# A decoder trunk on one core: attention scores three heads ahead, and products with the values behind the next head's transposes, first parts first

## The chip, the cores and the metric

The kernel runs on one core of one Trainium2 chip. Times are device microseconds of one execution. The core has five engines that each run their own instructions in a fixed order: TensorE (PE, matmuls; PEld are its weight loads), VectorE (DVE), ScalarE (ACT), GpSimd (POOL) and SyncE (SP, which issues the DMA transfers).

## The reference, cut to what matters

The program is a trunk of two decoder layers over 512 positions of width 1024. The first layer mixes a gated MLP (half A) and eight heads of stick-breaking attention (half B), projects both halves with one matrix, and is followed by a squared-ReLU MLP; the second layer uses an mLSTM. The change is in the attention of the first layer only:

```python
def _stick_breaking(q, k, v):              # (1, 8 heads, 512, 64)
    scale = q.shape[-1] ** -0.5
    for blk in range(seq // 128):
        t0, t1 = blk * 128, blk * 128 + 128
        z = jnp.einsum('bhtd,bhsd->bhts', q[:, :, t0:t1], k[:, :, :t1]) * scale
        mask = jnp.arange(t1)[None, :] < jnp.arange(t0, t1)[:, None]
        log1m = jnp.where(mask, -jax.nn.softplus(z), 0.0)
        suffix = lax.cumsum(log1m, axis=3, reverse=True)
        a = jnp.where(mask, jnp.exp(z + suffix), 0.0)
        outs.append(jnp.einsum('bhts,bhsd->bhtd', a, v[:, :, :t1]))

def _even_mixer(h, w_in, w_out, ...):
    ...                                     # y_a: gated MLP; q, k normed, v from p = h @ w_in
    o = _stick_breaking(q, k, v)
    return jnp.concatenate([y_a, y_b], axis=-1) @ w_out
```

## The kernel before

Everything is in float32. A matmul operand is carried as two parts, a first part `hi` (written by ACT) and a second part `lo`, the rest (written by DVE as source minus `hi`); a product is then three matmuls (`mm3`: hi by hi, lo by hi, hi by lo), and the helper `split` makes the parts. Weights come by DMA in tiles of 128 x 1024 (`w_load`), are split by ACT (`wh`, L189) and by DVE or, for tiles 14 to 29, by POOL (`wl`, L190), and five split tiles are held.

The attention works head by head. `head_scores(h)` transposes q (for two heads at once) and k into PSUM banks of tag B and splits them into `qs`, `kh` and `kl`; then, for the four blocks of 128 queries from the last to the first, it forms the scores `z` in a B bank (L530 to L532). ACT takes two sigmoids of it: `m`, of minus z (L535), and `a`, of z (L536). DVE runs a product scan backwards over `m` (L537) and multiplies `a` by the shifted scan (L540; by DVE for the last block of queries, by POOL for the other three). For a head the scans are 512, 384, 256 and 128 wide.

`head_out(h, aa)` then transposes the pieces of `a` into banks of tag C (L554), in three steps: key block j = 0, j = 1, and j = 2 and 3 together. Each step is split into `hi` and `lo` (L286, L287). These parts lie in two sets of buffers: even heads use three blocks of `xhi` and `xlo`, odd heads `ath1` and `atl1`. The products with the values go to the one bank of tag O (L567), for each key block the first part and then the second. The output is gathered (`ot`, L573 and L574) and split once more: the first part by ACT (L576), the second, `yl`, by POOL (L577).

While attention runs, PE is given filler work: `w_out_pieces` multiplies half A, which is ready, by the output matrix, in 32 pieces of three matmuls (banks of tag A, operands `yah` and `yal`); after every four pieces, that is twelve matmuls, DVE adds the finished block to the residual `xres` (L587). The function `step`, called behind certain matmuls of the attention, counts a quarter for each call, and at every full one it issues a piece. What is left over runs behind the attention, ahead of the product of half B with the output matrix (operands `vc`, `xlo`, `xhi`).

The calls are written in this order: scores of heads 0 and 1, the V projection, then for each head the scores of the next but one head and the output of this one. A scheduler that runs when the program is built takes the written order as priorities and fixes the order on each engine; where operands or buffers are not free, work that was written later can stand earlier.

Of the kernel before, what the change touches and what calls it, by code (L numbers as in the profile page):

```python
# [12 lines left out]
F32 = mybir.dt.float32  # L13
# [6 lines left out]
P = 128  # L20
T = 512
NT = 4
# [110 lines left out]
def _program(ctx, tc, nc, I, O):  # L133
    pool = lambda n, b=1: ctx.enter_context(tc.tile_pool(name=n, bufs=b))
    act, dve, pe, gp = nc.scalar, nc.vector, nc.tensor, nc.gpsimd
    f = lambda t: t.bitcast(F32)
# [9 lines left out]
    def bank(tag, dt=F32):  # L146
        cnt[0] += 1
        return ps.tile([P, 512], dt, name=f"ps{tag}{cnt[0]}", tag=f"ps{tag}", bufs=NB[tag])
# [86 lines left out]
    def w_take(n, la=LA):  # L235
        a = wpos[0]
        wpos[0] += n
        while len(wq) < wpos[0] + la:
            if next(units, units) is units:
                break  # L240
        return wq[a:a + n]
# [13 lines left out]
    def tts(t):  # L255
        return slice(t * P, (t + 1) * P)
# [24 lines left out]
    def split_scaled(dhi, dlo, src, g):  # L281
        act.activation(dhi, src, AF.Copy, scale=g)
        dve.scalar_tensor_tensor(dlo, src, g, f(dhi), op0=ALU.mult, op1=ALU.subtract)  # L283

    def split(dhi, dlo, src):
        act.activation(dhi, src, AF.Copy)  # L286
        dve.tensor_tensor(dlo, src, f(dhi), op=ALU.subtract)  # L287
# [161 lines left out]
    with ExitStack() as ax:  # L449
        ap = ax.enter_context(tc.tile_pool(name="at", bufs=1))  # L450
        qn = [ap.tile([P, 512], F32, name=f"qn{t}") for t in range(NT)]
        kn = [ap.tile([P, 1024], F32, name=f"kn{t}") for t in range(NT)]
        vc = ap.tile([P, NT, 8, 2, 64], F32R, name="vc")
# [4 lines left out]
        AO = (0, 512, 896, 1152)  # L458
        fl = lambda a: a[:, 0:3, :].rearrange("p k t -> p (k t)")
        ath = [fl(xhi), ap.tile([P, 1408], F32R, name="ath1")]  # L460
        atl = [fl(xlo), ap.tile([P, 1408], F32R, name="atl1")]
# [26 lines left out]
        def tok_transpose(src, c0):  # L488
            c = bank("B")
            for t in range(NT):  # L490
                i = pe.transpose(c[:, tts(t)], src[t][:, c0:c0 + P], ident)
            step(i)
            return c
# [5 lines left out]
        def step(ins):  # L499
            acc[0] += RATE if fill else 0  # L500
            if acc[0] >= 1:
                acc[0] -= 1
                with tc.issue_after(ins.ins):
                    next(fill[0], None)

        def head_scores(h):
            if h % 2 == 0:
                c = tok_transpose(qn, h * 64)
                for e in range(2):
                    es = slice(64 * e, 64 * e + 64)  # L510
                    qs = ap.tile([P, 512], F32R, name=f"qs{h + e}", tag="qs", bufs=3)
                    act.activation(qs[:64], c[es], AF.Copy, scale=pc("qng")[es])
                    dve.scalar_tensor_tensor(qs[64:], c[es], pc("qng")[es], f(qs[:64]), op0=ALU.mult, op1=ALU.subtract)
                    qst[h + e] = qs
            qs = qst[h]
            c = tok_transpose(kn, h * P)
            kh = ap.tile([P, 512], F32R, name=f"kh{h}", tag="kh", bufs=2)
            kl = ap.tile([P, 512], F32R, name=f"kl{h}", tag="kl", bufs=2)
            split_scaled(kh, kl, c, kng8)
            aa = [None] * NT  # L520
            z01 = None
            for tb in (3, 2, 1, 0):
                if tb > 1:
                    z = bank("B")
                else:
                    z01 = z01 if z01 is not None else bank("B")
                    z = z01[:, tb * 256:(tb + 1) * 256]
                n = P * (tb + 1)
                w = max(n, 256)
                pe.matmul(z[:, :w], lhsT=qs[:, tts(tb)], rhs=kh[:, :w], start=True, stop=False)  # L530
                pe.matmul(z[:, n - P:n], lhsT=identb, rhs=maskb[:, :P], start=False, stop=False)
                step(pe.matmul(z[:, :w], lhsT=qs[:, tts(tb)], rhs=kl[:, :w], start=False, stop=True))  # L532
                m = ap.tile([P, n], F32, name=f"m{h}_{tb}", tag=f"m{tb}", bufs=1)
                a = ap.tile([P, n], F32, name=f"a{h}_{tb}", tag=f"a{tb}", bufs=2)
                act.activation(m, z[:, :n], AF.Sigmoid, scale=-1.0)  # L535
                act.activation(a, z[:, :n], AF.Sigmoid)  # L536
                dve.tensor_tensor_scan(m[:, ::-1], m[:, ::-1], ones.to_broadcast([P, n]), 1.0,  # L537
                                       op0=ALU.mult, op1=ALU.mult)
                eng = dve if tb == 3 else gp
                eng.tensor_tensor(a[:, :n - 1], a[:, :n - 1], m[:, 1:n], op=ALU.mult)  # L540
                aa[tb] = a
            return aa
# [1 line left out]
        ones = ap.tile([P, 1], F32, name="ones")  # L544
        gp.memset(ones, 1.0)

        def head_out(h, aa):
            hi, lo = ath[h % 2], atl[h % 2]
            for js in ((0,), (1,), (2, 3)):
                c = bank("C")  # L550
                n = 0
                for j in js:
                    for tb in range(j, NT):
                        i = pe.transpose(c[:, n:n + P], aa[tb][:, j * P:(j + 1) * P], ident)  # L554
                        n += P
                step(i)
                if len(js) == 1:
                    split(hi[:, AO[j]:AO[j] + n], lo[:, AO[j]:AO[j] + n], c[:, :n])
                else:
                    split(hi[:, 896:1152], lo[:, 896:1152], c[:, :256])  # L560
                    split(hi[:, 1280:1408], lo[:, 1280:1408], c[:, 256:384])
            o = bank("O")
            for j in range(NT):
                t0 = min(j, 2) * P
                v2 = vc[:, j, h].rearrange("p e d -> p (e d)")
                for i, w in enumerate((hi, lo)):
                    x_ = pe.matmul(o[:, t0:], lhsT=v2, rhs=w[:, AO[j]:AO[j] + T - t0], start=j == 0 and i == 0,  # L567
                                   stop=j == NT - 1 and i == 1)
                step(x_)
            pr = slice((h % 2) * 64, (h % 2) * 64 + 64)  # L570
            yh, yl = yb(h // 2, 0)[pr], yb(h // 2, 1)[pr]
            ot = junk.tile([P, T], F32, name=f"ot{h}", tag="jk", bufs=1)[pr]
            act.activation(ot, o[64:], AF.Copy)  # L573
            dve.tensor_tensor(ot, o[:64], ot, op=ALU.add)  # L574
            oc = ot.rearrange("p (t c) -> p t c", t=NT)
            act.activation(yh, oc, AF.Copy)  # L576
            gp.tensor_tensor(yl, oc, f(yh), op=ALU.subtract)  # L577

        def w_out_pieces(hus):

            for d in range(KT):
                for k in range(4):
# [4 lines left out]
                        dve.tensor_tensor(xs[:, d, :], b, xs[:, d, :], op=ALU.add)  # L587
                    yield

        pend = [head_scores(0), head_scores(1)]  # L590
        act_chunk(w_take(4, LAV), 2, 512, v_evac, itertools.cycle("A"))
        pieces = w_out_pieces(w_take(4, 0))
        fill[:] = [pieces]
        for a in ath + atl:
            gp.memset(f(a[:, 1152:1280]), 0.0)
        for h in range(8):
            if 2 <= h + 1 < 8:
                pend.append(head_scores(h + 1))
            head_out(h, pend.pop(0))
        fill.clear()  # L600
        for _ in pieces:
            pass
# [336 lines left out]
```

## Time and profile before

| | |
|---|---|
| median of 3 runs | 1137.15 us (1135.97 to 1138.31) |
| profiled execution | 1138.17 us, its span 1136.4 us |
| PE busy | 1105.9 us (97%), 6372 matmuls |
| DVE busy | 825.9 us (73%) |
| ACT busy | 523.9 us (46%) |
| POOL busy | 163.9 us (14%) |
| granted PE clock | 0.994 over the span |

Rows of the timeline give the start in the span, the duration, engine, line, operation, the tiles written and read, shapes, and in brackets how long the engine stood idle before and what ended that. A matmul's duration holds its pipeline, so the distance from one start to the next is what it costs in a run of matmuls. Where a row is marked x2, two operations of one form are merged.

### The profile page before, as it was taken

How to read it: one execution, taken by the hardware profiler on the slowest of the kernel's cores; microseconds unless marked ns; L12 is line 12 of the kernel's file. 1: busy time of each engine (PE TensorE's matmuls, PEld its weight loads, DVE VectorE, ACT ScalarE, POOL GpSimd, SP SyncE). 2: the span in 40 equal slices, each digit the busy share in tenths (PEclk: the TensorE clock that was granted, in tenths of full speed). 3: DMA queues.
4: the chain of work that ended last, by engine and by line, in shares of the span. 5: the costliest groups of instructions: out<-in, count | busy, mean ns of one | idle time of the engine just before them, and what ended most of it. 6: DMA issues, size and time to landing. Idle time of an engine off the chain costs nothing.

```text
span 1136.4 us, 15912 instructions
## 1 busy us (share of the span) xinstructions
PE 1105.9 (97%) x6372; PEld 959.9 (84%) x6372; DVE 825.9 (73%) x1135; ACT 523.9 (46%) x800; POOL 163.9 (14%) x154
## 2 busy tenths in 40 slices
PE   7899989999999999999999999999999999999998
PEld 5788767878988988988988888887899899899898
DVE  7753599468957957857977677679887677677685
ACT  5343577445435435435555444435543444444441
POOL 7316564540000000000030010003100000000000
PEclk9899999999999999999999999999999999999999
DMA  7222310242241241251042203204324224224121
GB/s 231 92 75 76 105 43 1 74 169 91 94 133 71 97 138 64 93 149 56 20 130 77 93 20 112 93 25 155 118 74 140 83 74 147 76 75 149 37 84 65
DMA packets 34506, 105.18 MB, mean 93 GB/s; under 512 B 3712, under 2 KB 10112, under 8 KB 34432
## 3 DMA queue, kind: packets, MB, share of 16 engines
q1 hardware_dynamic: 34432, 104.17, 28.4%
q8 instruction: 50, 0.82, 0.3%
q14 instruction: 24, 0.20, 0.1%
HBM read 102.06 MB, written 2.10 MB: 92 GB/s over the span
## 4 chain that ended last, share of the span: by engine, by line
PE 79%; DVE 13%; ACT 2%; issue 2%; POOL 2%; DMA 2%; SPq 0%; DVEq 0%; ACTq 0%; POOLq 0%
PE psA L292 10%; PE psA L290 10%; PE psA L291 10%; PE psB L676 7%; PE psB L674 7%; PE psB L675 7%; PE psC L291 5%; PE psC L292 5%; PE psC L290 5%; DVE m L537 2%; DVE wl L190 2%; PE psO L290 2%; PE psO L291 2%; PE psO L292 2%; DVE xlo L283 1%
## 5 line engine op out<-in xcount | busy, mean ns | idle before, releaser
L189 ACT ACTIVATE wh<-wr 128x1024 fp32r<-128x1024 f32 (+1 forms) x124 | 131.3, 1061 | 173.3 <-DMA wr<-wall 53.1
L190 DVE TENSOR_TENSOR wl<-wr,wh 128x1024 fp32r<-128x1024 f32 (+1 forms) x108 | 136.6, 1271 | 84.4 <-ACT wh L189 54.2
L189 ACT ACTIVATE wh<-wq_s 128x1024 fp32r<-128x1024 f32 x64 | 67.2, 1060 | 125.3 <-PE psC L291 57.8
L291 PE MATMUL psA<-xlo,wh 128*128 128x512 f32 x292 | 115.2, 394 | 0.0
L292 PE MATMUL psA<-xhi,wl 128*128 128x512 f32 x288 | 114.1, 396 | 0.5 <-DVE wl L190 0.5
L290 PE MATMUL psA<-xhi,wh 128*128 128x512 f32 x288 | 112.6, 392 | 1.1 <-DVE xres L327 1.1
L291 PE MATMUL psC<-xlo,wh 128*128 128x512 f32 x256 | 102.1, 399 | 0.0
L292 PE MATMUL psC<-xhi,wl 128*128 128x512 f32 x256 | 102.0, 399 | 0.0
L290 PE MATMUL psC<-xhi,wh 128*128 128x512 f32 x256 | 101.2, 395 | 0.0
L292 PE MATMUL psA<-wh,xlo 128*128 128x512 f32 (+2 forms) x232 | 87.7, 380 | 4.0 <-DVE xlo L283 2.2
L290 PE MATMUL psA<-wh,xhi 128*128 128x512 f32 (+2 forms) x232 | 88.4, 383 | 1.8 <-ACT wh L189 1.7
L189 ACT ACTIVATE wh<-wq 128x1024 fp32r<-128x1024 f32 x48 | 50.9, 1060 | 85.2 <-PE psB L675 35.1
L291 PE MATMUL psA<-wl,xhi 128*128 128x512 f32 (+2 forms) x232 | 87.7, 379 | 1.1 <-DVE wl L190 1.1
L190 DVE TENSOR_TENSOR wl<-wq_s,wh 128x1024 fp32r<-128x1024 f32 x64 | 77.5, 1219 | 3.5 <-ACT wh L189 2.5
L339 POOL TENSOR_TENSOR ssq<-ssq,sq 128x512 f32<-128x512 f32 x18 | 28.8, 1600 | 351.8 <-ACT sq L338 351.8
L725 DVE SCALAR_TENSOR_TENSOR r<-psC,rrow 128x512 f32<-128x512 f32 x32 | 22.1, 690 | 60.8 <-PE psC L292 60.8
L290 PEld LDWEIGHTS psA<-xhi,wh 128*128 128x128 f32 x288 | 54.7, 190 | 13.8 <-ACT sq L338 1.5
L291 PEld LDWEIGHTS psA<-xlo,wh 128*128 128x128 f32 x292 | 54.9, 188 | 12.2
L686 DVE TENSOR_TENSOR xres<-xres,psB 128x512 f32<-128x512 f32 x80 | 53.9, 681 | 15.4 <-PE psB L676 14.8
L292 PEld LDWEIGHTS psA<-xhi,wl 128*128 128x128 f32 x288 | 54.1, 188 | 12.2 <-DVE wl L190 0.8
L190 DVE TENSOR_TENSOR wl<-wq,wh 128x1024 fp32r<-128x1024 f32 x48 | 58.6, 1221 | 2.6 <-ACT wh L189 2.3
L290 PEld LDWEIGHTS psC<-xhi,wh 128*128 128x128 f32 x256 | 48.9, 191 | 11.1
(396 smaller groups left out, 3147.4 us busy)
## 6 DMA issues: line engine op xcount, KB each, us to landing
wr<-wall SPq DMA_DIRECT2D x122, 512.0 KB, 3.5
wq<-wall SPq DMA_DIRECT2D x64, 512.0 KB, 3.9
out<-xres SPq DMA_DIRECT2D x16, 128.0 KB, 1.8
wr<-wv SPq DMA_DIRECT2D x2, 528.0 KB, 3.5
xres<-xT SPq DMA_DIRECT2D x4, 256.0 KB, 5.7
xres<-xT SPq DMA_DIRECT2D x2, 512.0 KB, 8.6
lngb<-lngb SPq DMA_DIRECT2D x1, 512.0 KB, 5.4
sgr<-sgw SPq DMA_DIRECT2D x1, 512.0 KB, 6.2
```

Of the source, the lines that this page charges most:

```text
L189: act.activation(hi[:, :n], raw, AF.Copy)
L190: (gp if i in POOL_LO else dve).tensor_tensor(lo[:, :n], raw, f(hi[:, :n]), op=ALU.subtract)
L290: pe.matmul(out, lhsT=lh, rhs=rh, start=first, stop=False)
L291: pe.matmul(out, lhsT=lh, rhs=rl, start=False, stop=False)
L292: pe.matmul(out, lhsT=ll, rhs=rh, start=False, stop=last)
L339: (dve if i == KT - 1 else gp).tensor_tensor(ssq, ssq, j, op=ALU.add)
L537: dve.tensor_tensor_scan(m[:, ::-1], m[:, ::-1], ones.to_broadcast([P, n]), 1.0, op0=ALU.mult, op1=ALU.mult)
L674: pe.matmul(o, lhsT=lh, rhs=rh, start=first, stop=False, skip_group_check=True)
L675: pe.matmul(o, lhsT=lh, rhs=rl, start=False, stop=False, skip_group_check=True)
L676: pe.matmul(o, lhsT=ll, rhs=rh, start=False, stop=fin, skip_group_check=True)
L686: add = lambda dst, b, op=ALU.add: dve.tensor_tensor(dst, dst, b, op=op)
L725: dve.scalar_tensor_tensor(r, b, 0.0, rb[0], op0=ALU.max, op1=ALU.mult)
```

## The change

Scores now run three heads ahead (`pend` begins with heads 0, 1 and 2), for which `a` has four buffers for each block in place of two. `head_out` is cut in two: `head_parts(h)` makes the transposes and their parts, `head_out(h)` the products and the output. The products of head h - 1 are written behind the transposes of head h and the scores of head h + 3. In the products, all first parts of the four key blocks come first, then all second parts, and `step` is called behind every second matmul.

```diff
-                a = ap.tile([P, n], F32, name=f"a{h}_{tb}", tag=f"a{tb}", bufs=2)
+                a = ap.tile([P, n], F32, name=f"a{h}_{tb}", tag=f"a{tb}", bufs=4)
...
-        def head_out(h, aa):
+        def head_parts(h, aa):
             hi, lo = ath[h % 2], atl[h % 2]
...
+        def head_out(h):
+            hi, lo = ath[h % 2], atl[h % 2]
             o = bank("O")
-            for j in range(NT):
-                t0 = min(j, 2) * P
-                v2 = vc[:, j, h].rearrange("p e d -> p (e d)")
-                for i, w in enumerate((hi, lo)):
-                    x_ = pe.matmul(o[:, t0:], lhsT=v2, rhs=w[:, AO[j]:AO[j] + T - t0], start=j == 0 and i == 0,
-                                   stop=j == NT - 1 and i == 1)
-                step(x_)
+            for i, w in enumerate((hi, lo)):
+                for j in range(NT):
+                    t0 = min(j, 2) * P
+                    x_ = pe.matmul(o[:, t0:], lhsT=vc[:, j, h].rearrange("p e d -> p (e d)"), rhs=w[:, AO[j]:AO[j] + T - t0],
+                                   start=j == 0 and i == 0, stop=j == NT - 1 and i == 1)
+                    if j % 2:
+                        step(x_)
...
-        pend = [head_scores(0), head_scores(1)]
+        pend = [head_scores(h) for h in range(3)]
...
         for h in range(8):
-            if 2 <= h + 1 < 8:
-                pend.append(head_scores(h + 1))
-            head_out(h, pend.pop(0))
+            head_parts(h, pend.pop(0))
+            if h + 3 < 8:
+                pend.append(head_scores(h + 3))
+            if h:
+                head_out(h - 1)
+        head_out(7)
```

In the rows below, a name ends in the number of the tile; psO is the bank of a head's products, psB that of scores or of transposed q and k, psC of transposes of `a`, psA of the fillers (`yah`, `yal`). The first difference on PE stands behind the V projection, at head 0's products. Before, the rows ahead of head 2's first score are:

```order
L554 MATMUL psC90_1215<-ident_84,a0_2_1006 128x128
L554 MATMUL psC90_1215<-ident_84,a0_3_996 128x128 x2
L567 MATMUL psO91_1223<-xlo_73,vc_648 128x512
L290 MATMUL psA92_1226<-yah_95,wh20_827 128x512
L291 MATMUL psA92_1226<-yal_96,wh20_827 128x512
L292 MATMUL psA92_1226<-yah_95,wl20_828 128x512
L567 MATMUL psO91_1223<-xhi_72,vc_648 128x384
L290 MATMUL psA92_1226<-yah_95,wh21_833 128x512
L291 MATMUL psA92_1226<-yal_96,wh21_833 128x512
L292 MATMUL psA92_1226<-yah_95,wl21_834 128x512
L567 MATMUL psO91_1223<-xlo_73,vc_648 128x384
L530 MATMUL psB95_1264<-kh2_1260,qs2_1249 128x512
```

After, at the same place (the last two of head 0's first transposes follow its first products):

```order
L569 MATMUL psO109_1424<-xhi_72,vc_648 128x512
L569 MATMUL psO109_1424<-xhi_72,vc_648 128x384
L554 MATMUL psC95_1274<-ident_84,a0_2_1006 128x128
L554 MATMUL psC95_1274<-ident_84,a0_3_996 128x128 x2
L530 MATMUL psB86_1098<-kh2_1094,qs2_1083 128x512
L531 LDWEIGHTS identb_89
L531 MATMUL psB86_1098<-maskb_91,identb_89 128x128
L532 MATMUL psB86_1098<-kl2_1095,qs2_1083 128x512
```

A second part and six fillers stood between head 0's last transposes and head 2's scores (psB95 before, psB86 after), and stand there no more.

Further on, PE reaches the score product of head 7 with its second weight part, `kl7`. Before, the next rows are:

```order
L532 MATMUL psB141_1754<-kl7_1751,qs7_1648 128x512
L530 MATMUL psB142_1767<-kh7_1750,qs7_1648 128x384
L531 LDWEIGHTS identb_89
L531 MATMUL psB142_1767<-maskb_91,identb_89 128x128
L532 MATMUL psB142_1767<-kl7_1751,qs7_1648 128x384
L530 MATMUL psB143_1777<-kh7_1750,qs7_1648 128x256
L531 LDWEIGHTS identb_89
L531 MATMUL psB143_1777<-maskb_91,identb_89 128x128
L532 MATMUL psB143_1777<-kl7_1751,qs7_1648 128x256
L567 MATMUL psO138_1727<-ath1_651,vc_648 128x512
L567 MATMUL psO138_1727<-atl1_652,vc_648 128x512
L567 MATMUL psO138_1727<-ath1_651,vc_648 128x384
```

Ahead of them four filler blocks of twelve are complete (psA92, psA102, psA115, psA127), and head 5's products follow, first and second part in turn. After:

```order
L532 MATMUL psB133_1673<-kl7_1670,qs7_1568 128x512
L530 MATMUL psB134_1683<-kh7_1669,qs7_1568 128x384
L531 LDWEIGHTS identb_89
L531 MATMUL psB134_1683<-maskb_91,identb_89 128x128
L532 MATMUL psB134_1683<-kl7_1670,qs7_1568 128x384
L290 MATMUL psA135_1687<-yah_95,wh20_827 128x512
L291 MATMUL psA135_1687<-yal_96,wh20_827 128x512
L292 MATMUL psA135_1687<-yah_95,wl20_828 128x512
L290 MATMUL psA135_1687<-yah_95,wh21_833 128x512
L291 MATMUL psA135_1687<-yal_96,wh21_833 128x512
L292 MATMUL psA135_1687<-yah_95,wl21_834 128x512
L290 MATMUL psA135_1687<-yah_95,wh22_1139 128x512
```

Ahead of these only three blocks are complete (psA97, psA110, psA122); the fourth, psA135, stands behind the product with `kl7`.

On DVE, the place is head 4. Before, from its first scan (`m4_3`) on:

```order
L537 SCALAR_TENSOR_TENSOR m4_3_1466<-m4_3_1466,ones_969 128x512
L540 TENSOR_TENSOR a4_3_1467<-a4_3_1467,m4_3_1466 128x511
L537 SCALAR_TENSOR_TENSOR m4_2_1480<-m4_2_1480,ones_969 128x384
L287 TENSOR_TENSOR xlo_73<-psC109_1413,xhi_72 128x128
L537 SCALAR_TENSOR_TENSOR m4_1_1490<-m4_1_1490,ones_969 128x256
```

After:

```order
L537 SCALAR_TENSOR_TENSOR m4_3_1385<-m4_3_1385,ones_969 128x512
L590 TENSOR_TENSOR xres_74<-psA97_1287,xres_74 128x512
L540 TENSOR_TENSOR a4_3_1386<-a4_3_1386,m4_3_1385 128x511
L537 SCALAR_TENSOR_TENSOR m4_2_1395<-m4_2_1395,ones_969 128x384
L287 TENSOR_TENSOR xlo_73<-psC113_1455,xhi_72 128x128
L537 SCALAR_TENSOR_TENSOR m4_1_1409<-m4_1_1409,ones_969 128x256
```

The residual add (xres) now stands among the scans, ahead of `a4_3`; before it stood elsewhere, behind the 128-wide scan or between splits. The adds of the next two blocks stand among the scans of heads 5 and 6 in the same way. At head 2, DVE's order from the second scan to the third is now `m2_2`, one split (`atl1`), `m2_1`; before, `a2_3` and two splits stood between them.

## The prediction

> **What bounds the kernel now.** The page shows TensorE (PE) busy 97% of the span, so I first looked for the stretch where it is not: the busy time of each engine by stretch over the attention heads. Columns: stretch, its length, then PE, PE weight loads, VectorE (DVE), ScalarE (ACT), GpSimd (POOL), granted PE clock, DMA.
>
> ```profile
> core 0: us, PE busy (x) PEld busy (x) DVE busy (x) ACT busy (x) POOL busy (x), PEclk, DMA share, GB/s
> 138.11:150.00 11.89, 9.16 (x51) 7.53 (x49) 10.11 (x13) 8.71 (x19) 8.29 (x6) 0.86 0.45 134
> 150.00:188.28 38.28, 33.37 (x206) 26.75 (x204) 37.31 (x59) 30.81 (x75) 18.37 (x18) 1.00 0.05 15
> 188.28:198.90 10.62, 10.24 (x54) 7.95 (x54) 10.11 (x17) 6.85 (x19) 6.25 (x7) 1.00 0.01 2
> 200.00:210.00 10.00, 10.00 (x50) 8.33 (x49) 3.87 (x7) 4.88 (x8) 3.96 (x3) 1.00 0.00 0
> 210.00:220.00 10.00, 10.00 (x46) 8.12 (x45) 1.38 (x2) 3.35 (x4) 8.23 (x4) 1.00 0.52 159
> ```
>
> From 138.11 to 188.28 us DVE is busy 10.11 + 37.31 = 47.42 of 50.17 us, and PE only 42.53. DVE sets the pace there, with 2.75 us of idle time of its own. From 200 us PE is busy all the time and DVE is not. The right edge, 188.28, is the end of `kl` of head 7, the last weight split that a score product waits for. Next, in the timeline of PE, who ends its waits:
>
> ```profile
> 144.22 0.90 PE L554 MATMUL psC<-ident,a 128*128 128x128 f32 x3 [2.73 <-DVE xlo L287]
> 152.60 0.39 PE L567 MATMUL psO<-xlo,vc 128*128 128x256 f32 x1 [1.06 <-DVE xlo L287]
> 160.07 0.39 PE L567 MATMUL psO<-atl,vc 128*128 128x256 f32 x1 [1.12 <-DVE atl L287]
> 168.41 0.39 PE L567 MATMUL psO<-xlo,vc 128*128 128x256 f32 x1 [0.70 <-DVE xlo L287]
> 177.28 0.39 PE L567 MATMUL psO<-atl,vc 128*128 128x256 f32 x1 [0.83 <-DVE atl L287]
> 186.56 0.39 PE L567 MATMUL psO<-xlo,vc 128*128 128x256 f32 x1 [0.73 <-DVE xlo L287]
> 188.40 0.50 PE L532 MATMUL psB<-kl,qs 128*128 128x512 f32 x1
> ```
>
> Six waits of 0.70 to 2.73 us end on a DVE split. Five of them (1.06 + 1.12 + 0.70 + 0.83 + 0.73 = 4.44 us) hold a head's last second-part product. The row at 188.40 is the product with head 7's `kl`; after it PE hardly waits again. So the end of this stage is: the time at which DVE finishes head 7's `kl`, plus all PE work that stands behind that point in PE's order. That is the sum I make. A wait of PE ahead of it is slack; work of PE ahead of it is free.
>
> **The work put behind that point.** The change moves the marks after which filler pieces (`w_out_pieces`, three matmuls each) are issued: fewer marks are passed by a given score, and the order shows it. Ahead of the product with head 7's `kl`, both orders hold the same transposes, scores and products with values of heads 0 to 4; only the fillers differ, 48 matmuls before (four output blocks complete), 36 now (three). The other 12 now stand right behind. Their price, from a run of nine on a busy PE:
>
> ```profile
> 183.48 0.39 PE L290 MATMUL psA<-yah,wh 128*128 128x512 f32 x1
> 185.56 0.28 PE L567 MATMUL psO<-xhi,vc 128*128 128x256 f32 x1
> ```
>
> Nine fillers take 185.56 - 183.48 = 2.08 us, 0.231 each, so 12 cost **+2.77 us** at the end of the stage: before, they filled time in which PE waited anyway, and that time now stays empty. Their cover would be a wait of PE behind the point; before there is none of note, and now the two j = 2,3 transposes of head 6 are the only candidate, which I put at 0 to 1 us and take as 0. If PE did not have to wait at that point at all, the 12 would cost nothing.
>
> **Scores three heads ahead.** In PE's order the first row that differs stands behind the V projection and head 0's first products; head 2's transposes were there already. The extra two buffers of `a` therefore move no work under the V projection: 0, and no ACT, SP or DMA row ahead of this point differs.
>
> **Products behind the next transposes, first parts first.** Here DVE could gain. These are its rows that matter, with the PE and ACT rows that led to the second gap:
>
> ```profile
> 144.67 0.74 DVE L513 SCALAR_TENSOR_TENSOR qs<-psB,par,qs 64x512 fp32r<-64x512 f32 x1
> 145.44 0.75 DVE L283 SCALAR_TENSOR_TENSOR kl<-psB,kng,kh 128x512 fp32r<-128x512 f32 x1
> 147.15 0.76 DVE L513 SCALAR_TENSOR_TENSOR qs<-psB,par,qs 64x512 fp32r<-64x512 f32 x1
> 149.50 2.14 DVE L537 TENSOR_TENSOR_SCAN m<-m,ones 128x512 f32<-128x512 f32 x2 [1.58 <-ACT m L535]
> 172.87 1.93 DVE L537 TENSOR_TENSOR_SCAN m<-m,ones 128x512 f32<-128x512 f32 x1 [0.38 <-ACT m L535]
> 187.63 0.72 DVE L283 SCALAR_TENSOR_TENSOR kl<-psB,kng,kh 128x512 fp32r<-128x512 f32 x1
> 148.28 0.48 PE L532 MATMUL psB<-kl,qs 128*128 128x512 f32 x1
> 148.87 0.60 ACT L535 ACTIVATE m<-psB 128x512 f32<-128x512 f32 x1 [2.61 <-PE psB L532]
> ```
>
> DVE idled 1.58 us before head 2's first scan, since PE had first waited until 144.22, then done a second part and six fillers. Now head 2's scores stand directly behind the transposes. They need `qs` (done 145.41) and `kl` (done 146.19); adding the product, 0.48, and the sigmoid, 0.60, the scan's input is there at 147.3, before DVE ends the `qs` row at 147.91. By this wait alone the gain would be 1.58 us. But GpSimd is in the way. Scans and the POOL rows over which they stretched:
>
> ```profile
> 138.11 2.57 DVE L537 TENSOR_TENSOR_SCAN m<-m,ones 128x512 f32<-128x512 f32 x1 [4.27 <-ACT m L535]
> 156.60 2.05 DVE L537 TENSOR_TENSOR_SCAN m<-m,ones 128x512 f32<-128x512 f32 x2
> 164.96 1.55 DVE L537 TENSOR_TENSOR_SCAN m<-m,ones 128x512 f32<-128x512 f32 x1
> 182.77 2.95 DVE L537 TENSOR_TENSOR_SCAN m<-m,ones 128x512 f32<-128x512 f32 x2
> 190.58 1.20 DVE L537 TENSOR_TENSOR_SCAN m<-m,ones 128x512 f32<-128x512 f32 x1
> 134.84 4.77 POOL L190 TENSOR_TENSOR wl<-wr,wh 128x1024 fp32r<-128x1024 f32 x2 [1.26 <-ACT wh L189]
> 147.31 2.39 POOL L190 TENSOR_TENSOR wl<-wr,wh 128x1024 fp32r<-128x1024 f32 x1
> 151.81 1.13 POOL L540 TENSOR_TENSOR a<-a,m 128x383 f32<-128x383 f32 x1 [2.10 <-ACT m L535]
> 156.28 4.64 POOL L577 TENSOR_TENSOR xlo<-ot,vc 64x512 fp32r<-64x512 f32 x1
> 164.14 1.30 POOL L577 TENSOR_TENSOR xlo<-ot,vc 64x512 fp32r<-64x512 f32 x1 [0.96 <-ACT vc L576]
> 172.44 1.28 POOL L577 TENSOR_TENSOR vc<-ot,vc 64x512 fp32r<-64x512 f32 x1 [1.36 <-ACT vc L576]
> 182.51 1.28 POOL L577 TENSOR_TENSOR vc<-ot,vc 64x512 fp32r<-64x512 f32 x1 [1.65 <-ACT vc L576]
> ```
>
> A 512-wide scan takes 1.20 us (190.58). At 138.11 it took 2.57, and the POOL pair that was running ended at 139.61: the scan stood still until POOL was done. The same at 164.96 (+0.35), 172.87 (+0.73) and 182.77 (2.95 against the 2.05 at 156.60 for the same two scans, +0.90), each with `yl` of a head (L577) running; at 156.28 the scan won, and `yl` took 4.64. The weight split at 147.31 runs until 149.70, and POOL's order ahead of it is unchanged. The scan would start under it at 147.9 and end at 149.70 + 1.20 = 150.90, against 150.70 now. I take **+0.20**, with -1.58 as the other end if POOL does not hold it. I take the former because POOL began 0.6 us earlier, as in the row at 138.11.
>
> The Trainium skill, "SBUF — State Buffer", section "Who interferes with whom", has the rule: a DVE instruction with two SBUF inputs and a GpSimd instruction that reads SBUF share one read interface, and whichever issues first blocks the other for its whole length. By that rule the sum below stands, by the wait row alone it would be 1.78 lower; the trace agrees with the rule (2.57 against 1.20).
>
> The gap of 0.38 ahead of 172.87 followed a PE held up by the product at 168.41; that wait is gone, so **-0.38**, at most all idle left, -0.97 from 150 on.
>
> **Where the POOL work falls.** Two things change in DVE's order that the rows price. For head 2, `a` x `m` on POOL (1.13 us, 151.81) is released by the second scan; behind that scan DVE now does one split, then the third scan:
>
> ```profile
> 152.46 0.68 DVE L287 TENSOR_TENSOR atl<-psC,ath 128x512 fp32r<-128x512 f32 x1
> 170.44 0.67 DVE L587 TENSOR_TENSOR xres<-psA,xres 128x512 f32<-128x512 f32 x1
> ```
>
> The split's slot is 0.60 (152.46 to 153.06), so the third scan meets POOL's operation and waits about 0.5. And `yl` of heads 1, 2 and 3: the residual add (0.67 at 170.44, slot 0.60) now stands between scans of the next heads and takes one input from PSUM. The `yl` that lost at 156.28 got through only once DVE was past its scans and at such PSUM work, so a waiting `yl` (1.28, as at 172.44) can start beside the add and hold the next scan for 0.68 each. That is 0.5 + 3 x 0.68 = 2.54 against the 0.35 + 0.73 + 0.90 = 1.98 of before: **+0.56**. Bounds: all stalls gone, -1.98; four `yl` and four `a` x `m` blocking in full, 4 x 1.28 + 4 x 0.5 = 7.1, +5.1.
>
> **The sum.** 2.77 + 0.20 - 0.38 + 0.56 = +3.15 us. The profiled execution took 1138.17 (span 1136.4, 1.77 around it), 1.02 above the median 1137.15; it would become 1141.3, and the median **1140.3**. Everything behind the stage moves with it, if the next weights are still split in time:
>
> ```profile
> 214.04 2.40 POOL L190 TENSOR_TENSOR wl<-wr,wh 128x1024 fp32r<-128x1024 f32 x1
> 220.92 0.62 PE L292 MATMUL psA<-vc,wl 128*128 128x512 f32 x2
> ```
>
> The last of these splits ends on POOL at 216.44 and is first read at 220.92, 4.5 us later. The chain of loads ahead of it starts when a filler frees a buffer; in PE's order the distance from that filler to this first read shrinks from 70 rows to 63, at 0.231 by 1.6 us. So it stays hidden; if the 4.5 us were gone it would cost up to 1.6.
>
> **Rivals.**
> 1. *The gap closes.* Head 2's scan wins against POOL as at 156.28, and DVE gains 1.58 and 0.38: 2.77 - 1.96 = +0.8, 1138.0, no change. The row at 138.11 speaks against, the one at 156.28 for. With some stalls gone too, it goes to 1137.
> 2. *PE gets its waits back: faster.* The five waits on second parts are what the new order removes, and if PE is the bound in this stage it gains them: 1137.15 - 4.44 = 1132.7. It decides if DVE can end head 7's `kl` more than 2.77 + 2.27 = 5.0 us earlier; DVE's idle (2.75) and stalls (1.98) together are 4.7, so nearly all of both must go.
> 3. *More stalls.* DVE and POOL meet at every head, and the j = 2,3 transposes of head 6 wait 1 us behind them: +3 more, 1143.3.
> 4. *Half the clock.* The stretch from 138.11 had a granted clock of 0.86, behind the idle 2.73 us at 144.22. PE has less to do there now, and a longer slow stretch would make scores late; before 154 us they wait for `kl` of head 3 anyway, so +0 to +1.
>
> "TensorE: Matmul & The Clock Gate" in the Trainium skill, section "Why this matters for your kernels", warns of idle gaps above about 3 us; the 2.73 us here came with a drop already.
>
> **Chances and range.** A measurement of this kernel tells about 0.2%, 2.27 us, from no change: 1134.88 to 1139.42. My forecast with rivals 3 and 4 gives slower: 0.57 (the sum 0.40, rival 3 0.12, rival 4 0.05). Rival 1 and small errors of the sum give no change: 0.35. Rival 2, 0.08. The range goes from 1137.0 (rival 1 with half of the stalls gone) to 1143.5 (rival 3).
>
> **What would show it.** In the new trace PE should sit idle about 3 us more in all between 138 and head 7's `kl`, which should end within 1 us of 188.3 from the same start, with 12 fillers right behind its product; no PE wait on the last second part; the scan of head 2 stretched to some 2.9 us under the POOL split. If head 7's `kl` ends by 186, rival 1 or 2 holds, and the DVE steps were wrong; if the 12 fillers show waits behind them, the 2.77 was covered.

## The result and the profile after

The changed kernel takes 1142.03 us (median of 8 runs, 1139.37 to 1144.7); the kernel before, run beside it, 1136.56 (1133.43 to 1138.83). The ratio is 1.0050, 95% interval 1.0037 to 1.0064, that is +5.7 us (+4.2 to +7.3). It is slower, as forecast, by more than the +3.15 of the sum. The profiled execution took 1142.96 us, its span 1141.2.

Below, "front" is the stretch from the start of head 1's first scan to the start of head 7's `kl`, and "tail" the one from there to the first instruction behind the attention's output product. Ahead of the front both kernels do the same, though this execution reached it 2.05 us earlier (over the 14 kernels of this study that start lies between 134.56 and 138.11); behind the tail both need 915 us. First front, tail and both together before, then after, in the view of busy times by stretch with the prediction's columns:

```profile
138.11:187.63 49.52, 41.88 (x251) 33.91 (x250) 46.76 (x70) 38.89 (x90) 26.23 (x23) 0.97 0.14 43
187.63:221.35 33.72, 33.34 (x165) 26.93 (x163) 16.70 (x28) 15.92 (x33) 19.42 (x13) 1.00 0.19 55
138.11:221.35 83.24, 75.22 (x413) 60.84 (x412) 63.46 (x96) 54.81 (x122) 45.65 (x36) 0.98 0.16 48
```

```profile
136.06:189.17 53.11, 41.87 (x237) 33.25 (x236) 50.98 (x69) 38.92 (x90) 25.05 (x23) 0.93 0.12 40
189.17:225.88 36.71, 36.71 (x177) 30.36 (x177) 16.03 (x28) 16.03 (x33) 17.91 (x13) 0.96 0.13 44
136.06:225.88 89.82, 78.58 (x413) 63.61 (x412) 67.01 (x96) 54.96 (x122) 42.96 (x36) 0.94 0.13 42
```

Two readings of the same rows. By DVE: the front grew by 3.59 us, since DVE is busy 4.22 us longer in it for the same kind of work and idle 0.63 us less; the tail grew by 2.99, with twelve more matmuls in it (177 for 165). By PE: over both, PE does the same 413 matmuls, and the whole grew by 6.58 us, of which 3.36 is busy time (75.22 to 78.58) and 3.22 time in which PE is not busy (8.02 to 11.24). PE's clock is lower, 0.94 for 0.98: matmuls that are the same took longer. In the front DVE sets the pace (idle 2.76 us before, 2.13 after), in the tail PE does (idle 0.38 and 0.00), so the end is counted by DVE's time in the front and by PE's in the tail. PE's waits in its timeline after:

```profile
142.17 0.55 PE L554 MATMUL psC<-ident,a 128*128 128x128 f32 x3 [2.39 <-DVE xlo L287]
155.77 0.66 PE L554 MATMUL psC<-ident,a 128*128 128x128 f32 x4 [1.18 <-POOL a L540]
167.92 0.65 PE L554 MATMUL psC<-ident,a 128*128 128x128 f32 x3 [1.25 <-DVE xlo L287]
178.40 0.55 PE L554 MATMUL psC<-ident,a 128*128 128x128 f32 x3 [1.58 <-DVE atl L287]
188.11 0.55 PE L554 MATMUL psC<-ident,a 128*128 128x128 f32 x3 [2.10 <-DVE xlo L287]
190.34 0.78 PE L532 MATMUL psB<-kl,qs 128*128 128x512 f32 x1
191.79 0.55 PE L290 MATMUL psA<-yah,wh 128*128 128x512 f32 x1
194.75 0.28 PE L530 MATMUL psB<-kh,qs 128*128 128x256 f32 x1
```

No wait stands at a last second-part product any more. In its place PE waits ahead of transposes: four of the five waits end on a DVE split, since two banks of tag C take turns and the split of the block before last still holds the one that is needed; the fifth, at 155.77, ends on POOL's `a` x `m`. The row at 190.34 is the product with head 7's `kl`; the twelve fillers run from 191.79 to 194.75. Why DVE is later, in its timeline and POOL's:

```profile
145.86 2.83 DVE L537 TENSOR_TENSOR_SCAN m<-m,ones 128x512 f32<-128x512 f32 x1
149.52 0.95 DVE L537 TENSOR_TENSOR_SCAN m<-m,ones 128x384 f32<-128x384 f32 x1
150.97 1.06 DVE L537 TENSOR_TENSOR_SCAN m<-m,ones 128x256 f32<-128x256 f32 x1
156.22 2.61 DVE L537 TENSOR_TENSOR_SCAN m<-m,ones 128x384 f32<-128x384 f32 x2
165.10 0.67 DVE L590 TENSOR_TENSOR xres<-psA,xres 128x512 f32<-128x512 f32 x1
165.68 1.13 DVE L540 TENSOR_TENSOR a<-a,m 128x511 f32<-128x511 f32 x1
167.78 0.67 DVE L537 TENSOR_TENSOR_SCAN m<-m,ones 128x256 f32<-128x256 f32 x1
172.70 1.23 DVE L537 TENSOR_TENSOR_SCAN m<-m,ones 128x512 f32<-128x512 f32 x1 [1.30 <-ACT m L535]
174.64 2.03 DVE L537 TENSOR_TENSOR_SCAN m<-m,ones 128x384 f32<-128x384 f32 x1
177.18 0.98 DVE L537 TENSOR_TENSOR_SCAN m<-m,ones 128x256 f32<-128x256 f32 x1
183.16 3.11 DVE L537 TENSOR_TENSOR_SCAN m<-m,ones 128x512 f32<-128x512 f32 x2
186.78 1.07 DVE L540 TENSOR_TENSOR a<-a,m 128x511 f32<-128x511 f32 x1
145.23 2.37 POOL L190 TENSOR_TENSOR wl<-wr,wh 128x1024 fp32r<-128x1024 f32 x1
150.62 0.87 POOL L540 TENSOR_TENSOR a<-a,m 128x383 f32<-128x383 f32 x1 [3.02 <-DVE m L537]
155.74 1.70 POOL L580 TENSOR_TENSOR xlo<-ot,vc 64x512 fp32r<-64x512 f32 x1
164.43 1.84 POOL L580 TENSOR_TENSOR xlo<-ot,vc 64x512 fp32r<-64x512 f32 x1 [2.37 <-ACT vc L579]
174.49 1.36 POOL L580 TENSOR_TENSOR vc<-ot,vc 64x512 fp32r<-64x512 f32 x1 [3.91 <-ACT vc L579]
183.75 1.70 POOL L580 TENSOR_TENSOR vc<-ot,vc 64x512 fp32r<-64x512 f32 x1 [2.37 <-ACT vc L579]
```

`yl` is L580 here. Alone, the scans take 1.20 (512 wide), 0.95 (149.52) and 0.67 (167.78), and `a` x `m` on DVE about 0.67. Each long row lies over a POOL instruction that was running or came in between, and ends behind it. The four `yl` of the front lengthen DVE rows by 2.61 - 0.95 - 0.67, 1.13 - 0.67, 2.03 - 0.95 and 3.11 - 1.20 - 0.95, about 3.5 us in all; before it was 1.98. `a` x `m` on POOL adds 0.39 (150.97), 0.31 (177.18) and 0.40 (186.78), 1.1 us.

On DVE the front adds up: head 2's first scan is 1.63 us longer, beside POOL's weight split (2.83 for 1.20), and the idle 1.58 us ahead of it is gone; POOL's other work lengthens rows by 3.5 + 1.1 = 4.6 us, 2.6 more than before; the gap ahead of head 5's first scan (172.70) is 1.30 us, 0.92 more than before. That is 1.63 - 1.58 + 2.6 + 0.92 = 3.57 of the 3.59.

### The profile page after: what moved, and what is told of

The parts are those of the page before. It is cut to its first block, busy times and chain, and to the rows that moved or that the text cites. A ratio compares the mean times of both kernels' runs of the same rounds, so it can differ in the third digit from the quotient of the medians.

```text
span 1141.2 us, 15902 instructions
## 1 busy us (share of the span) xinstructions
PE 1110.7 (97%) x6372; PEld 963.5 (84%) x6372; DVE 827.9 (73%) x1135; ACT 524.3 (46%) x800; POOL 160.2 (14%) x154
## 4 chain that ended last, share of the span: by engine, by line
PE 79%; DVE 10%; ACT 3%; POOL 3%; issue 3%; DMA 1%; SPq 0%; POOLq 0%; DVEq 0%; ACTq 0%
PE psA L290 10%; PE psA L292 10%; PE psA L291 10%; PE psB L682 7%; PE psB L680 7%; PE psB L681 7%; PE psC L291 5%; PE psC L292 5%; PE psC L290 5%; PE psO L290 2%; DVE wl L190 2%; PE psO L291 2%; PE psO L292 2%; DVE m L537 1%; DMA wr<-wall 1%
```

## What the clock does

The lower clock was found in the traces. Where it falls in front and tail, it falls to 0.50 for 3.41 us, in two kernels once for two times 3.41, and within one execution all such stretches start a whole number of 3.41 us apart (after: at 144.33, 168.23 and 188.71, 7 and 6 windows apart). So I cut the trace of after on that grid and looked at PE's busy time in the window ahead of each. In the view by stretch PE's busy time stands behind the length, and the clock third from the end:

```profile
140.92:144.33 3.41, 1.22 (x6) 0.73 (x7) 3.35 (x6) 2.73 (x6) 3.41 (x3) 1.00 0.00 0
144.33:147.74 3.41, 3.41 (x15) 2.90 (x16) 3.35 (x4) 2.65 (x7) 2.84 (x3) 0.50 0.55 155
164.82:168.23 3.41, 1.84 (x14) 1.32 (x12) 3.41 (x6) 2.60 (x8) 1.82 (x2) 1.00 0.01 2
168.23:171.64 3.41, 3.41 (x15) 2.49 (x13) 3.17 (x7) 1.47 (x3) 1.89 (x3) 0.50 0.02 5
175.06:178.47 3.41, 1.83 (x15) 1.49 (x14) 3.41 (x5) 2.00 (x6) 1.82 (x3) 1.00 0.01 2
178.47:181.88 3.41, 2.94 (x16) 2.01 (x17) 3.31 (x6) 2.82 (x6) 0.89 (x2) 1.00 0.00 0
185.30:188.71 3.41, 1.31 (x10) 0.98 (x8) 3.41 (x6) 1.09 (x4) 1.02 (x2) 1.00 0.00 0
188.71:192.12 3.41, 3.41 (x14) 2.67 (x13) 3.23 (x7) 2.76 (x7) 1.04 (x2) 0.50 0.00 0
```

A window in which PE was busy 1.22, 1.84 or 1.31 of 3.41 us is followed by one at half the clock; 1.83 sits on the edge and is not. I did the same for all 14 traces of this study, 364 windows over front and tail: of the windows at full clock, all 24 with PE busy 1.67 us or less were followed by half the clock, 4 of the 9 between 1.83 and 2.00, none above 2.00. The other two slow windows follow a slow one. So what matters is not how long one wait is but whether PE is busy for about half of a window: the wait of 1.25 us at 167.92 was followed by a slow window, since one of 0.33 us lay in the same window, and the one of 1.58 at 178.40 was not. These two windows are alike (1.84 and 1.83 busy), so on the edge PE's busy time does not decide, and nothing here shows what does. A slow window in which PE is never idle takes 1.71 us of its work. Before has one (at 143.93, behind the wait of 2.73), after three: 2 x 1.71 = 3.4, the 3.36 of busy time above.

The lower clock is no accident of the profiled execution: in all 8 runs of after the granted clock over the span was 0.988 to 0.990, in the 101 runs of before that stood beside the experiments 0.989 to 0.995, with a median of 0.994.

PE's lost work is not yet lost time. In the front it counts where it makes DVE wait: in after, as far as the rows show, that is the gap of 1.30 us at 172.70, behind the slow window from 168.23. In the tail PE sets the pace, and 2.95 us of the slow window from 188.71 lie there, at half the clock up to 1.5 us. Kernels with the same twelve fillers in the tail bear this out: with a slow window there the tail is 36.71 (after), 36.67 (parts interleaved) and 36.71 us (yl on DVE), without one 35.50 (after without yl).

The Trainium skill, "TensorE: Matmul & The Clock Gate", section "Part 1: The HAM clock gate", gives two clock rates, a half and the whole, and a free-running window of about 3.4 us; the trace agrees with both (0.50, 3.41). The warning of gaps above some 3 us on the same page of the Trainium skill, section "Why this matters for your kernels", weighed in the prediction, is too mild here: windows with waits of 1.25 to 2.39 us in them were followed by windows at half the clock.

## The experiments

Each kernel ran beside the kernel before, which is the base of every number here. Waits and busy time are those of PE in front and tail together against before, as above; "slow" is the number of windows at half the clock. The last three columns part front and tail, again against before, and give DVE's busy time in the front; what is left of the front is DVE's idle time.

| kernel | us against before (95%) | front and tail | waits | busy | slow | front | its DVE busy | tail |
|---|---|---|---|---|---|---|---|---|
| before | 0 | 83.24 | 8.02 | 75.22 | 1 | 49.52 | 46.76 | 33.72 |
| after | +5.7 (4.2 to 7.3) | +6.58 | +3.22 | +3.36 | 3 | +3.59 | +4.22 | +2.99 |
| depth alone | +1.9 (0.5 to 3.3) | +2.73 | +0.93 | +1.80 | 3 | +2.67 | +2.88 | +0.06 |
| deferral alone | +2.5 (0.9 to 4.1) | +3.25 | +1.61 | +1.64 | 2 | +1.95 | +2.04 | +1.30 |
| after, parts interleaved | +7.7 (5.7 to 9.8) | +6.54 | +4.08 | +2.46 | 3 | +3.59 | +3.37 | +2.95 |
| after, RATE 0.28 | +1.7 (0.3 to 3.1) | +2.68 | +2.21 | +0.47 | 1 | +2.26 | +4.16 | +0.42 |
| after without yl | +1.4 (-0.2 to 3.1) | +0.66 | -0.57 | +1.23 | 2 | -1.12 | +0.67 | +1.78 |
| before without yl | -1.8 (-3.3 to -0.2) | -2.81 | -1.69 | -1.12 | 1 | -2.04 | -1.86 | -0.77 |
| before, RATE 0.20 | +9.6 (7.2 to 11.9) | +8.89 | +5.18 | +3.71 | 3 | +5.14 | +4.06 | +3.75 |
| before, RATE 0.30 | +2.6 (1.1 to 4.1) | +3.27 | +0.52 | +2.75 | 3 | +3.05 | +1.57 | +0.22 |
| after, fillers at transposes | -1.3 (-2.8 to +0.5) | +0.28 | -1.30 | +1.58 | 3 | +0.54 | +1.57 | -0.26 |
| before, fillers at transposes | +0.6 (-1.0 to 2.2) | +1.30 | +1.44 | -0.14 | 1 | +1.90 | +3.30 | -0.60 |
| after, yl on DVE | +4.8 (3.0 to 6.6) | +5.34 | +3.21 | +2.13 | 2 | +2.35 | +4.10 | +2.99 |
| after, fillers at transposes, 1.2 | -1.6 (-3.3 to +0.1) | -0.64 | -1.70 | +1.06 | 2 | +2.35 | +1.09 | -2.99 |

What one profiled execution shows for front and tail lies within 1.6 us of the timed difference for every kernel, though the rest of the program is over 900 us long. DVE's busy time in the front is longer than before in every kernel but one, before without yl.

**Depth alone.** In the kernel before:

```diff
-a = ap.tile([P, n], F32, name=f"a{h}_{tb}", tag=f"a{tb}", bufs=2)
+a = ap.tile([P, n], F32, name=f"a{h}_{tb}", tag=f"a{tb}", bufs=4)
...
-pend = [head_scores(0), head_scores(1)]
+pend = [head_scores(h) for h in range(3)]
...
-    if 2 <= h + 1 < 8:
-        pend.append(head_scores(h + 1))
     head_out(h, pend.pop(0))
+    if h + 3 < 8:
+        pend.append(head_scores(h + 3))
```

> The kernel before with the scores three heads ahead (and four buffers of each a) alone; the products stay right behind their own head's transposes and keep their interleaved parts. In its order 42 filler matmuls stand ahead of head 7's product with kl, before 48. Theory of the fillers: 6 x 0.231 = +1.4 us against before. Theory of the stalls (yl of the deferred products on POOL against the scans): nothing more, since no yl is deferred: +1.0 to +2.0 in all. Rival, that the depth itself carries the loss: +4 to +6.

It cost +1.9, at the upper end of the fillers' theory. But the tail did not grow (33.78 for 33.72); the front did, by 2.67, with two more slow windows. The number came out and the reason did not. In the view by stretch, the front, and in DVE's timeline the rows that are longer:

```profile
135.77:187.96 52.19, 43.37 (x245) 34.92 (x243) 49.64 (x70) 39.81 (x93) 25.02 (x24) 0.90 0.13 41
155.16 1.52 DVE L540 TENSOR_TENSOR a<-a,m 128x511 f32<-128x511 f32 x1
163.73 3.68 DVE L537 TENSOR_TENSOR_SCAN m<-m,ones 128x512 f32<-128x512 f32 x3
167.34 1.28 DVE L540 TENSOR_TENSOR a<-a,m 128x511 f32<-128x511 f32 x1
175.60 1.35 DVE L537 TENSOR_TENSOR_SCAN m<-m,ones 128x256 f32<-128x256 f32 x1
```

DVE is busy 2.88 us longer (49.64 for 46.76) and idle 0.21 less. The first two rows lie beside a `yl` (on POOL from 154.65 and 164.15), the other two beside `a` x `m` on POOL (167.00 and 175.28); alone they take about 0.67, 2.82, 0.67 and 0.67. So scores that run further ahead move POOL's work among the scans without any `yl` being deferred, and these stalls are the front's growth. Its three slow windows do not show as idle time of DVE.

**Deferral alone.** In the kernel after:

```diff
-pend = [head_scores(h) for h in range(3)]
+pend = [head_scores(0), head_scores(1)]
...
 for h in range(8):
+    if 2 <= h + 1 < 8:
+        pend.append(head_scores(h + 1))
     head_parts(h, pend.pop(0))
-    if h + 3 < 8:
-        pend.append(head_scores(h + 3))
     if h:
         head_out(h - 1)
```

with two buffers of `a`.

> The kernel after with the scores again only one head ahead (two buffers of each a): the products still stand behind the next head's transposes, first parts first. In its order 48 fillers stand ahead of head 7's product with kl, as before. Theory of the fillers: 0 from them. Theory of the stalls: yl of each head falls among the next head's scans as it does after, +3. Both together +3. Rival, that the deferral is what helps (PE no longer waits for second parts: 4.44 us) and the depth loses: -1 to -4.

+2.5, as the stalls' theory has it, and DVE is busy 2.04 us longer in the front; the deferral does not help. Each half of the change costs some 2 us, all of it 5.7.

**The order of parts.** The products of after as they were before:

```diff
-for i, w in enumerate((hi, lo)):
-    for j in range(NT):
+for j in range(NT):
...
+    for i, w in enumerate((hi, lo)):
...
```

> The kernel after with the products' two parts interleaved again, key block by key block; 36 fillers stand ahead of head 7's product with kl, as after. The deferred products find both parts ready, so by both theories the order of parts is worth nothing: +5 to +6 against before, as after (1.005). Rival, that first parts first carries some of the loss or of a gain: outside +4.5 to +6.5.

+7.7: the median lies in the rival's range, but the interval reaches into both and overlaps that of after. It is unclear whether first parts first gain up to 2 us; that they carry some of the loss is not what this run shows.

**Fillers earlier in after.**

```diff
-RATE = 0.25
+RATE = 0.28
```

> The kernel after with RATE 0.28 in place of 0.25: 48 fillers stand ahead of head 7's product with kl in its order, after 36. Theory of the fillers: 12 x 0.231 = 2.8 us of the loss go, so +2.7 against before where after has +5.5. Rival, that fillers ahead of that product delay PE as much as behind it, or that the stalls make the whole loss: +5 to +6. Rival, that fillers fill PE's new waits and the scans too start later: above +6.

```profile
135.32:221.24 85.92, 75.69 (x413) 61.04 (x412) 66.92 (x97) 55.27 (x122) 41.51 (x36) 0.98 0.14 40
```

4.0 of the 5.7 us went; the forecast of +2.7 lies in the interval, so that it is more than the 2.8 of twelve fillers is not secured. By the profile the tail lost 2.57 of its 2.99 us and the front 1.33, nearly all of it idle time of DVE: DVE's stalls stayed (busy +4.16). The clock is at 0.98 again and PE's busy time within 0.47 of before, with one slow window in place of three. Waits, +2.21, remain.

**Without yl**, in after and in before:

```diff
-gp.tensor_tensor(yl, oc, f(yh), op=ALU.subtract)
```

> The kernel after with the instruction that writes yl (the second part of each head's sum, on POOL) left out, so its output is not the reference's. Theory of the stalls: in the trace of after the DVE rows that overlap a yl on POOL between head 1's first scan and head 7's kl are longer by 1.08 + 0.46 + 1.09 + 1.0 = 3.6 us; without yl these go and the kernel stands +2 (+1 to +3) against before. Rival, that the longer DVE rows only stand in slack that PE's waits would take anyway: +5 to +6, as after.

> The kernel before with yl left out in the same way (its output is not the reference's). Theory of the stalls: in the trace of before a yl lengthens DVE rows by 0.35 + 0.73 + 0.81 = 1.9 us in that stretch, so -1.9 (-3 to -1) against before; with the run of after without yl, the distance between the two kernels shrinks from 5.7 to about 4. Rival, slack: 0 for this kernel, and the distance stays 5.7.

-4.3 against after and -1.8 against before; 3.6 and 1.9 were read from the rows. The distance between the kernels shrinks from 5.7 to 3.2 us. Each of these differences is uncertain by some 1.5 us, so the times alone do not secure the 2.5; DVE's busy time in the front says the same, for without `yl` it falls by 3.55 us in after and by 1.86 in before. So some 2 us of the loss come from `yl` landing among the scans. In the view by stretch, the run of after without it:

```profile
135.00:218.90 83.90, 76.45 (x413) 62.20 (x412) 62.94 (x96) 55.07 (x122) 33.50 (x28) 0.96 0.14 45
```

DVE is busy 4.07 us less than in after (62.94 for 67.01), and PE's waits fall by 3.8: with DVE's stalls PE's waits go too.

**Fillers later and earlier in before**, RATE 0.20 and 0.30 in place of 0.25:

> The kernel before with RATE 0.20 in place of 0.25: 39 fillers stand ahead of head 7's product with kl in place of 48, nothing else is changed. Theory of the fillers: PE is full behind that product, so the 9 matmuls add 9 x 0.231 = +2.1 (+1.5 to +3). Rival, that fillers ahead of the product cost PE as much as behind it: 0 to +0.5.

> The kernel before with RATE 0.30: 60 fillers stand ahead of head 7's product with kl in place of 48. Theory of the fillers: PE idles 7.4 us between head 1's first scan and that product, which takes 12 x 0.231 = 2.8 us of fillers in, so -2.8 (-3.5 to -1.5), faster than before. Rival, that PE is late for the scores and the scans then wait: 0 to +2.

Both missed: +9.6 for +2.1, and +2.6 for -2.8. Here the theory that counts the fillers ahead of one product falls as an account of the whole. With RATE 0.20 three windows fell under the half. Its front and tail, and its three pairs of windows:

```profile
137.34:192.00 54.66, 43.70 (x241) 34.50 (x240) 50.82 (x69) 39.43 (x91) 26.34 (x23) 0.91 0.13 39
192.00:229.47 37.47, 35.23 (x174) 28.84 (x173) 16.67 (x28) 15.28 (x31) 18.55 (x13) 1.00 0.13 38
140.15:143.56 3.41, 0.69 (x5) 0.37 (x4) 3.41 (x6) 3.41 (x8) 1.83 (x3) 1.00 0.38 135
143.56:146.97 3.41, 3.41 (x11) 2.60 (x12) 3.31 (x6) 1.43 (x3) 2.98 (x3) 0.50 0.11 18
167.46:170.87 3.41, 1.47 (x12) 1.14 (x10) 3.41 (x5) 1.09 (x3) 2.42 (x3) 1.00 0.01 2
170.87:174.28 3.41, 3.35 (x11) 2.64 (x12) 2.98 (x7) 1.46 (x3) 0.71 (x2) 0.50 0.02 5
177.70:181.11 3.41, 1.25 (x7) 0.66 (x5) 3.38 (x6) 2.01 (x5) 2.55 (x3) 1.00 0.01 2
181.11:184.52 3.41, 3.23 (x9) 2.47 (x10) 2.89 (x6) 1.33 (x3) 0.00 (x0) 0.50 0.00 0
```

The tail grew by 3.75: nine fillers are 2.1 of it, and PE idles 1.86 us more there than before, so it was not full behind the product as expected. The front grew by 5.14, of which 1.08 is idle time of DVE and 4.06 busy time: the fillers moved, and with them the places where scans meet POOL. With RATE 0.30 PE's waits hardly changed (+0.52), and two more windows were slow. Here the rival's mechanism shows: nine fillers ran from 189.54 to 193.19, nearly all of it at half the clock, ahead of the product with head 7's `kl`, though that `kl` was ready at 189.47. The product came at 194.22, and DVE meanwhile stood idle for 2.99 us. So with fillers the place counts, and not the number alone.

**Fillers where PE waits.** In after, and in the same way in before, groups are counted at the transposes alone:

```diff
-def step(ins):
-    acc[0] += RATE if fill else 0
+def step(ins, rate=RATE):
+    acc[0] += rate if fill else 0
...
-step(i)                      # behind a block of transposes
+step(i, 1.0)
...                           # all other calls of step: rate 0
```

> The kernel after with one group of three fillers behind each of a head's three blocks of transposes and none elsewhere; 54 fillers stand ahead of head 7's product with kl. Theory of PE's waits and the clock (PE does the same work between head 1's first scan and the last head's sum in both kernels; after waits 3.2 us longer there and loses 3.4 us to stretches of low granted clock behind the waits): the groups fall into the waits for the split ahead of the next block (1.18, 1.25, 1.58, 2.10 us), both terms mostly go, -4 to -6 against after, so 0 to +1.5 against before. Theory of the stalls alone (the scans wait for yl on POOL, wherever fillers stand): +4 to +6 against before. Rival, that three fillers ahead of each block hold back transposes and scans: above +6.

> The kernel before with its fillers placed in the same way, behind the transposes and so ahead of the products that wait for second parts; 54 stand ahead of head 7's product with kl, before 48. Theory of PE's waits: its five waits ahead of products (4.44 us in all) are filled, -2 to -4 against before. Rival, that PE's waits are not what sets the end there and DVE's chain is: -0.5 to +2.

After gained some 7 us by it (-1.3 against before, rather better than forecast), before nothing (+0.6, the rival). The waits of after fall from +3.22 to -1.30. So the deferral and the depth are not slow as such: written as in after, but with the fillers at the transposes, the loss is gone. That it went because waits were filled is shown only in part: the tail is 3.25 us shorter than in after, with 54 fillers ahead of the product in place of 36, but in the front DVE is also busy 2.65 us less (48.33 for 50.98), as fewer of its rows are stretched beside POOL. In before the same move costs DVE 3.30 us more of busy time and saves it 1.40 of idle time. In before PE still waits 1.29, 0.97 and 0.69 us at last second parts, some rows behind the groups. After in this form:

```profile
134.56:218.08 83.52, 76.80 (x409) 62.04 (x408) 63.59 (x97) 54.71 (x122) 43.36 (x36) 0.94 0.17 48
```

It still has three slow windows (the clock 0.94), two of them early, behind the V projection, and gains in spite of them. (Four matmul records fewer than elsewhere: a few are missing from a trace.)

**yl on DVE**, in after:

```diff
-gp.tensor_tensor(yl, oc, f(yh), op=ALU.subtract)
+dve.tensor_tensor(yl, oc, f(yh), op=ALU.subtract)
```

> The kernel after with yl computed by DVE in place of POOL, same output. Theory of the stalls: 3.6 us of longer DVE rows go, and four yl of 0.68 us come on DVE in that stretch (+2.7), three more behind it where DVE has room: -0.9 against after, so +4 to +5.5 against before. Rival, that the lock has other POOL instructions behind it which then hold the scans instead: +7 to +9.

+4.8, as the stalls' theory had it; DVE trades stalls for work (busy 50.86 us in the front, 50.98 in after), and little is won.

**More fillers at the transposes**: 1.2 groups for each block in place of 1.0, and `while` for `if` where `step` counts.

> The kernel after with the fillers behind the blocks of transposes alone, as in the run before that, at 1.2 groups for each block in place of 1: 60 fillers stand ahead of head 7's product with kl in place of 54. Theory of PE's waits and the clock: PE there still waits 1.17 and 1.56 us ahead of blocks of heads 5 and 6, and the clock falls behind the second; six more fillers (1.4 us) fall into these waits: -1 to -2.5 against that kernel, so -2 to -4 against before. Rival, that DVE's chain now sets the end and more fillers only hold back its transposes: 0 to +3 against before.

-1.6 us, no better than with 1.0 as far as the runs tell. Both versions are the fastest ones here that compute the whole function, but their intervals reach to no change; that they beat before is not shown.

## Why the prediction was right or wrong

Slower was right, and 1142.03 lies in the range, 1.7 us above the 1140.3; but the loss is made of other terms than the sum has.

- **The shape of the sum** (DVE's end of head 7's `kl`, plus what PE has to do behind it) held as bookkeeping: front +3.59 where the sum has +0.20 - 0.38 + 0.56 = +0.38, tail +2.99 where it has 2.77, together 6.58 in the profiled execution.
- **Twelve fillers, +2.77:** the fillers stand where the order had them, and PE's listed waits up to the product grew from 7.43 to 10.85 us, the "about 3 us more". That the tail grew by 2.99 is in part luck: the slow window from 188.71 lies in it. Without one the same twelve fillers went with +1.78 (after without yl), and the other 1.2 went with the slow window. Why the fillers' net is under 2.77 is open, beyond the 0.38 us of idle time that they fill. As a cause for the whole the term was too simple (RATE 0.20 and 0.30).
- **Depth, 0:** wrong. PE's order ahead of head 0's products is the same, but the change of order behind it cost 1.9 us alone, by stalls: DVE is busy 2.88 us longer in the front.
- **Head 2's first scan, +0.20:** right. It took 2.83 us under POOL's weight split, as forecast, and ended 12.63 us behind the start of head 1's first scan, before 12.59.
- **The gap of 0.38 gone:** wrong; it is 1.30 (172.70). Head 5's scores and three fillers among them ran in the slow window from 168.23; at the full clock this work would have taken up to 1.7 us less, more than the gap. With one slow window (RATE 0.28) DVE's idle time in the front fell to 0.86 us in all.
- **POOL's stalls, +0.56:** the step that was mis-sized. I took one `a` x `m` and three `yl` at 0.68, each sharing its time with a residual add. The rows show three `a` x `m` (1.1) and four `yl` that meet the scans head on (3.5), 4.6 in place of 2.54, so about +2.6. The mechanism was right, rival 3 had the size: its +3 more. Leaving `yl` out moved the kernel by 4.3.
- **The clock, rival 4 at +0 to +1:** mis-sized as well. Two more slow windows took 3.36 us of PE's busy time; of that, as far as the rows show, the gap of 1.30 in the front and about 1.2 us in the tail reached the end. I asked only whether the slow stretch at 138 would grow, and not whether the idle time that I forecast for PE would make new ones.
- **Head 7's `kl` within 1 us of 188.3:** wrong by 3.6 (53.83 us from the common start to its end, before 50.24). The terms are those above: next to nothing from head 2's scan, stalls +2.6, the gap +0.92. (That the end stood at 188.28 before is a slight misreading: its row, 187.63 + 0.72, gives 188.35.)
- **Later weights hidden:** right, 915.05 us behind the tail before, 915.32 after.

Stalls, clock and fillers are not independent: with DVE's stalls gone PE's waits go, and windows that are half wait are followed by windows at half the clock. What stays open: where scans and POOL will meet after a change of order, which no term here foretells; why depth alone has two more slow windows with 0.93 us more of waits (one execution was profiled, and where the grid lies differs from one to the next); and how much of the scatter of a few us between runs comes from that. No run moved the grid.

## What to carry to other kernels

Find for each stretch the engine that sets the pace, and add up its busy and idle time there: here DVE's in the front, PE's in the tail. A change of order that moves no work onto that engine can still lengthen its rows, as POOL's work did here with DVE's scans in nearly every kernel; an instruction moved on POOL is priced by the DVE instructions that it will then run beside. Ask for every new wait of PE whether it leaves PE busy for less than half of a 3.41 us window: in these traces that took up to 1.71 us of PE's work in the next one, which is lost time where PE sets the pace or another engine waits for it. Put filler work where PE is seen to wait, and look again after each change of order: RATE 0.25 was better than 0.20 and 0.30 in before, and 0.28 better than 0.25 in after.

## What was not expected of the hardware

- PE's clock falls in whole windows of 3.41 us on a fixed grid, to 0.50, behind a window in which PE was busy less than about half of the time (24 of 24 at 1.67 us or less, 4 of 9 from 1.83 to 2.00, none above). Waits of 1.25 and 0.33 us in one window were enough, and one of 1.58 was not.
- DVE's residual add, which reads one input from PSUM, kept its 0.67 us at 165.10, with the `yl` of 164.43 running on POOL until 166.27; the product behind it, with both inputs in SBUF, took 1.13 in place of 0.67.
